# The feed-forward's projection back by seven products of sums, added up in shared PSUM banks

## The chip, the cores and the metric

The kernel runs on one core of one Trainium2 chip. The metric is the device time of one execution in microseconds (us); lower is better. All inputs and outputs are float32 in the chip's memory, and the kernel is one launch.

## The reference

One layer of a bidirectional encoder for 1024 tokens of width 1024: two token mixers, a SwiGLU feed-forward, a per-layer embedding, a final norm. What matters here is the feed-forward, with D_FF = 2816:

```python
h = rms_norm(x, g_ffn[i])
gt, up = split_cols(h @ w_gate_up[i], (D_FF, D_FF))
x = x + (jax.nn.silu(gt) * up) @ w_down[i]

pl = rms_norm(p[i] @ w_pl_proj[i], g_pl_proj[i])
x = x + jax.nn.sigmoid(rms_norm(x, g_pl[i]) @ w_pl_gate[i]) * pl
```

## The kernel before, in words

Everything is kept feature by token: a tile has 128 features on its partitions and 512 tokens (a token half) or 1024 along the free axis. To keep float32's precision, each operand is split into two float32r parts, hi and lo (`split`: ACT casts hi, DVE subtracts to get lo), and each 128x128 by 128x512 block is three products on TensorE: hi x hi, hi x lo, lo x hi (`mm3`). One PSUM bank holds one 128x512 result, and there are eight banks.

The block is written down as a list of instructions on stand-ins for tiles. `Plan.order` then gives them an order by list scheduling with estimated durations (which engine does what next, by level and place in the list, as inputs and buffers come free), and `Plan.run` issues them in that order. So no queue is written out by hand, and each engine runs its list strictly in order. Buffers are slots of pools: 32 large ones of 1024 columns (`big`), 8 and 4 of 512 (`mid`, `raw`), 6 for split weights (`w`, `N_W`), 8 banks.

Gate and up (`gate_up`, lines 1566 to 1602) already use Winograd's form of Strassen's product: the features, the tokens and the weights' columns (gate and up) are halves, and seven products of sums take the place of eight. Each of the 22 blocks of 128 hidden features takes seven products of four feature blocks (84 products on TensorE), each into a bank of its own; DVE then adds banks and intermediate results in SBUF (p1, u3, u4), ACT applies Silu, and the two token halves of the block go to memory (`d_hid`, 256 KB each). Block 0 is done plainly (`plain`), and blocks 1 to 4 have their first two products done early (`early`).

The projection back (`down`, lines 1640 to 1668) is plain. It runs over pieces of hidden blocks, `PIECES = (2, 4, 4, 1, 6, 5)`. For a piece it loads and splits both token halves of each block, then for each of eight 128-column blocks of the output loads and splits the weights (`load3`, four blocks to a tile) and, by token half, adds up the piece in one bank (`block_half`). DVE adds the bank to x, which stays in eight large tiles (`xT`). The last piece also splits x for the embedding and takes up its norm. Loads for this stage wait for the first half of hidden block 19 (`also=[d_hid[NF - 1 - X_AHEAD][0]]`).

While gate and up run, 28 of the 32 large slots hold the split sums of x; the first piece has two blocks because four slots are free before they end.

Of the kernel before, what the change touches and what calls it, by code (L numbers as in the profile page):

```python
# [14 lines left out]
F32R = mybir.dt.float32r  # L15
# [21 lines left out]
class Buf:  # L37
    """A stand-in for a tile."""
# [15 lines left out]
class View:  # L54
    """Part of a tile: partitions [p0, p1), free dimensions as (stride, size) from an offset."""
# [82 lines left out]
class Op:  # L138
# [7 lines left out]
# a DMA: from its issue to its data, and bytes in a microsecond  # L146
# [3 lines left out]
# from the end of an instruction to the start of one that needs it, by the engines of both  # L150
# [7 lines left out]
class VPool:  # L158
# [5 lines left out]
    def tile(self, shape, dtype=F32, tag=None, bufs=None, line=None, cap=99, stream=None):  # L164
        """line: tiles of a line are given out in the order of the program, at most cap at a time."""
# [7 lines left out]
class Plan:  # L173
# [11 lines left out]
    # -- recording  # L185
# [44 lines left out]
    # -- engines  # L230
    def matmul(self, out, lhsT, rhs, start, stop):
# [5 lines left out]
        o = self.add("pe", lambda: self.nc.tensor.matmul(out.ap(), lhsT.ap(), rhs.ap(), start=start, stop=stop),  # L237
# [96 lines left out]
    # -- scheduling  # L334
    def order(self):
# [6 lines left out]
        free_slots = {}     # (pool, tag) -> times at which slots come free  # L342
        queue = {}          # line -> tiles in program order
# [8 lines left out]
        wait = {e: [] for e in engs}       # heap by ready time: dependencies all scheduled  # L352
        avail = {e: [] for e in engs}      # heap by key: ready at the engine's time
# [19 lines left out]
        def slots_ready(o, now):  # L373
            """None when it can go now; else (time or None, (pool, tag))."""
# [20 lines left out]
        while len(done) < total:  # L395
# [43 lines left out]
            # worth the wait: something more urgent is about to be ready  # L439
# [62 lines left out]
    # -- issue  # L502
# [28 lines left out]
P = 128  # L531
# [25 lines left out]
# slots of each kind of tile, and what goes before what  # L557
# [4 lines left out]
PIECES = (2, 4, 4, 1, 6, 5)  # L562
# [17 lines left out]
# products of part 1 in order (k, q, v, g: glu, z, l: logits, p: per-layer embedding; with the head or  # L580
# block), and those that fill in
# [6 lines left out]
def ORDER(f):  # L588
    """The block up to the delta rule's end, in the order in which it is written down."""
# [10 lines left out]
def hybrid_block(tc, x, p, g_mix, w_in, conv_dw_w, conv_dw_b,  # L600
# [7 lines left out]
    big = pn.pool("big", N_BIG)          # 1024 columns and the padding of a convolution  # L608
    mid = pn.pool("mid", N_MID)          # 512 columns
# [30 lines left out]
    # ---------------------------------------------------------------- constants  # L640
# [46 lines left out]
    def load_w(w, r0, nk, c0, cap=4, pool=None):  # L687
        """nk blocks of 128 rows of w, 128 columns, split: by four blocks."""
# [17 lines left out]
    def mm3(ps, ah, al, bh, bl, start, stop):  # L706
        pn.matmul(ps, ah, bh, start, False)
        pn.matmul(ps, ah, bl, False, False)
        pn.matmul(ps, al, bh, False, stop)

    def block_half(w, acts, h, nk):
        """128 columns of w against 512 tokens: a bank of [column, token]."""
# [18 lines left out]
    def rows(r, n):  # L731
        """[P, n] values by token as a bank whose rows all hold them along the free axis."""
# [5 lines left out]
    def sums(acc, n):  # L738
        """Sums over partitions of acc's columns, token on the partition."""
# [5 lines left out]
    # ---------------------------------------------------------------- part 1  # L745
# [4 lines left out]
    # vectors by feature: rows of 128, transposed together  # L750
# [15 lines left out]
    # RMSNorm of x, transposed; x itself transposed  # L766
# [56 lines left out]
    # logits of decay and beta  # L823
    d_g = dp.tile([P, P], tag="dg", bufs=1)

    def logits():
# [26 lines left out]
        # log1p(e) = ln(u) - ((u - 1) - e) / u with u = 1 + e  # L853
# [135 lines left out]
    # ---------------------------------------------------------------- the delta rule  # L989
# [21 lines left out]
    def group(g):  # L1011
# [6 lines left out]
        for hh in range(2):  # L1018
# [14 lines left out]
            # by token: 1/|k|^2, |k|, and what the writes are scaled with  # L1033
# [7 lines left out]
            # decays between the tokens of a chunk: the direction that runs from partition to column has  # L1041
            # the sum of its logs <= 0, the other one >= 0
# [15 lines left out]
            # N (both directions in one matrix) and P  # L1058
# [23 lines left out]
        # inverses of the 32x32 diagonal blocks, one block to a partition  # L1082
# [35 lines left out]
    def head(g, hh, v, N, kT, nrm, b_, zt, ssq):  # L1118
        hd = 2 * g + hh
        # the inverses of 128x128 (eu: backward, forward) and their transposes (et: forward, backward)  # L1120
# [5 lines left out]
        for q4 in range(2):  # L1126
# [15 lines left out]
            # only the blocks beside the diagonal blocks are used of each product  # L1142
# [4 lines left out]
            # columns of px: blocks 0, 1, 2, 3, each in the direction that has it here  # L1147
# [17 lines left out]
        # v, scaled by |k|  # L1165
# [14 lines left out]
        # the chunks in order, both directions side by side  # L1180
# [585 lines left out]
```

## Time and profile before

| what | us |
|---|---|
| runs | 2145.12, 2142.41, 2143.38 |
| median of the runs | 2143.38 |
| profiled execution, first to last instruction (span) | 2144.9 |
| gate and up, from their first weights' load to the last weights' load | 1333.4 to 1730.6 |
| projection back, loads of its weights | 1737.2 to 1998.3 |

The profiled execution's own time is given as its span alone; it lies within the range of the runs. Line 237 is `matmul` and line 282 `_vec`, the helpers that record nearly every product and DVE instruction, and lines 259 and 266 are ACT's, so instructions are told apart by tile names: `ps` is a bank, `w` split weights, `big` a large tile, `raw` and `mid` weights as loaded or intermediate results, `m` and `lnb` intermediate results of 512 columns.

### The profile page before, as it was taken

The numbers are of one execution on the slowest core, as the hardware profiler recorded it, in microseconds if no ns is written. First come the engines' busy times: TensorE is split into PE (matmuls) and PEld (weight loads), VectorE is DVE, ScalarE is ACT, GpSimd is POOL, SyncE is SP. The second block draws the span as 40 slices with busy tenths as digits, with TensorE's granted clock in tenths as the row PEclk, the third lists the DMA queues.
The fourth block names the chain that finished last, engine by engine and source line by source line (L and its number), as shares of the span: only waits on it lengthen the run. The fifth ranks groups of instructions, "written<-read, shape, count | busy, mean of one in ns | idle before, by whom it ended". The sixth has DMA issues, their size and how long they took to land.

```text
span 2144.9 us, 29696 instructions
## 1 busy us (share of the span) xinstructions
PE 2094.7 (98%) x10434; PEld 1736.6 (81%) x10434; DVE 1606.4 (75%) x2621; ACT 1089.8 (51%) x2501; POOL 129.5 (6%) x203
## 2 busy tenths in 40 slices
PE   7999999999999999999999999999999999999998
PEld 5888788878888788878888888888888888888888
DVE  4488999977898989887687868786666667452676
ACT  6636656756656655767775435533323334121542
POOL 1000201110100111011100000000000000000000
PEclk9999999999999999999999999999999999999999
DMA  6233224522423422635468687432222227231253
GB/s 213 100 123 127 84 81 138 187 79 79 138 89 120 146 74 79 197 122 182 157 213 254 195 262 229 123 99 84 80 78 84 84 80 273 67 95 39 66 170 108
DMA packets 289077, 278.69 MB, mean 130 GB/s; under 512 B 17209, under 2 KB 217074, under 8 KB 288928
## 3 DMA queue, kind: packets, MB, share of 16 engines
q1 hardware_dynamic: 288928, 276.79, 40.3%
q8 instruction: 82, 1.34, 0.3%
q14 instruction: 67, 0.55, 0.1%
HBM read 198.02 MB, written 78.71 MB: 129 GB/s over the span
## 4 chain that ended last, share of the span: by engine, by line
PE 86%; ACT 7%; DVE 5%; issue 1%; DMA 1%; SPq 0%; POOL 0%; DVEq 0%; POOLq 0%; ACTq 0%
PE ps L237 84%; ACT big L259 4%; DVE big L282 3%; PE ps L242 2%; DVE mid L282 1%; ACT big L266 1%; ACT m L266 1%; DVE w L282 1%; ACT w L259 1%; DMA big<-in_x_dram 1%; DMA d<-mid 0%; ACT mid L266 0%; SPq L330 0%; ACT L266 0%; ACT mid L259 0%
## 5 line engine op out<-in xcount | busy, mean ns | idle before, releaser
L237 PE MATMUL ps<-big,w 128*128 128x512 f32 (+1 forms) x7524 | 1848.7, 399 | 0.9 <-ACT w L259 0.8
L237 PEld LDWEIGHTS ps<-big,w 128*128 128x128 f32 x7524 | 1383.4, 189 | 305.3 <-ACT w L259 1.2
L282 DVE SCALAR_TENSOR_TENSOR big<-big,cw 128x1024 f32<-128x1024 f32 x336 | 434.2, 1299 | 17.3 <-ACT big L266 12.3
L259 ACT CAST w<-raw 128x512 fp32r<-128x512 f32 (+2 forms) x340 | 198.3, 589 | 365.0 <-PE ps L237 288.4
L282 DVE TENSOR_TENSOR w<-raw,w 128x512 fp32r<-128x512 f32 (+2 forms) x340 | 221.6, 659 | 124.9 <-ACT w L259 119.3
L282 DVE TENSOR_TENSOR big<-ps,big 128x512 f32<-128x512 f32 (+1 forms) x132 | 89.9, 687 | 86.4 <-PE ps L237 76.2
L259 ACT CAST w<-mid 128x512 fp32r<-128x512 f32 x125 | 77.2, 621 | 149.5 <-PE ps L237 109.5
L282 DVE TENSOR_TENSOR w<-mid,w 128x512 fp32r<-128x512 f32 x125 | 85.9, 688 | 62.3 <-ACT w L259 61.6
L237 PEld LDWEIGHTS ps<-big 128*128 128x128 f32 x784 | 101.9, 195 | 16.1 <-issue 9.1
L237 PE MATMUL ps<-big 128*128 128x128 f32 (+1 forms) x784 | 107.2, 283 | 7.7 <-ACT big L259 5.1
L282 DVE TENSOR_TENSOR big<-big 128x512 fp32r<-128x512 f32 (+2 forms) x159 | 107.0, 707 | 8.7 <-ACT big L259 8.4
L259 ACT COPY big<-big 32x128 f32<-32x128 f32 (+1 forms) x264 | 102.5, 440 | 16.5 <-DVE big L282 12.5
L259 ACT COPY big<-ps 32x128 f32<-32x128 f32 (+3 forms) x162 | 66.8, 413 | 64.3 <-PE ps L237 55.0
L259 ACT CAST big<-big 128x512 fp32r<-128x512 f32 x120 | 69.9, 619 | 42.5 <-DVE big L282 21.3
L242 PE MATMUL ps<-ident,big 128*128 128x128 f32 (+1 forms) x432 | 72.0, 280 | 13.6 <-DMA big<-in_x_dram 9.3
L237 PEld LDWEIGHTS ps<-S,big 128*128 128x128 f32 x448 | 71.8, 190 | 10.0 <-DVE S L282 0.2
L237 PE MATMUL ps<-S,big 128*128 128x128 f32 x448 | 75.0, 275 | 0.0
L242 PEld LDWEIGHTS ps<-ident,big 128*128 128x128 f32 (+1 forms) x432 | 53.9, 147 | 25.2 <-issue 13.4
L237 PEld LDWEIGHTS ps<-big,m 128*128 128x128 f32 x512 | 64.1, 195 | 12.2 <-ACT m L266 9.4
L237 PE MATMUL ps<-big,m 128*128 128x128 f32 x512 | 66.1, 280 | 6.4 <-ACT m L266 6.3
L266 ACT ACTIVATE mid<-mid 128x512 f32<-128x512 f32 (+2 forms) x87 | 50.2, 580 | 38.6 <-DVE mid L282 26.8
L266 ACT ACTIVATE big<-big 128x1024 f32<-128x1024 f32 (+2 forms) x80 | 56.6, 715 | 22.2 <-DVE big L282 17.2
(158 smaller groups left out, 1711.0 us busy)
## 6 DMA issues: line engine op xcount, KB each, us to landing
d<-mid SPq DMA_DIRECT2D x162, 256.0 KB, 3.0
raw<-in_w_in_dram SPq DMA_DIRECT2D x128, 256.0 KB, 3.0
mid<-d SPq DMA_DIRECT2D x120, 256.0 KB, 3.4
big<-d SPq DMA_DIRECT2D x92, 256.0 KB, 4.0
big<-dqkv SPq DMA_DIRECT2D x32, 512.0 KB, 4.9
raw<-in_w_gate_up_dram SPq DMA_DIRECT2D x50, 256.0 KB, 2.9
dqkv<-big SPq DMA_DIRECT2D x24, 512.0 KB, 2.9
mid<-in_w_gate_up_dram SPq DMA_DIRECT2D x46, 256.0 KB, 4.0
```

Source lines behind the costliest of these rows:

```text
L237: o = self.add("pe", lambda: self.nc.tensor.matmul(out.ap(), lhsT.ap(), rhs.ap(), start=start, stop=stop), [out], [lhsT, rhs], cost)
L242: self.add("pe", lambda: self.nc.tensor.transpose(out.ap(), in_.ap(), ident.ap()), [out], [in_, ident], 0.107)
L259: return self.nc.scalar.copy(out.ap(), in_.ap())
L266: return self.nc.scalar.activation(out.ap(), in_.ap(), func, **kw)
L282: return getattr(e, name)(**{k: v.ap() if isinstance(v, View) else v for k, v in kw.items()})
```

## The change

The projection back takes the seven products too, for hidden blocks 0 to 17 as nine pairs (`NS = 9`), in three groups of three pairs (`PAIRS = (3, 3, 3)`); blocks 18 to 21 stay plain, as the last piece. The halves are the even and odd blocks of the pairs (features), the token halves, and two neighbouring 128-column blocks of the output.

- `hidden`: when both blocks of a pair are done, DVE takes four differences in place, and the seven forms (11, T1, T2, 21, T3, 22, T4) go to memory, 256 KB each, where four halves went before.
- `down_sums`: per group, 7 x 3 forms are loaded and split into large tiles (`df`, at most 24), then for four pairs of output blocks the four weight parts (three blocks, 384 columns) are loaded, four sums of weights are taken, and seven split weights give seven products of nine TensorE products each.
- Shared banks: T2, T3 and T4 are added into the bank that holds product 11, and 22 into that of T1. Between two products into one bank DVE adds it to x (`onto`): seven additions per pair.
- `gate_up` for blocks 5 to 21 shares banks in the same way (four banks, `pb`, `pc`, `pd` and none for the rest): ACT copies `pb` out three times between its products, and the additions on DVE that the bank now makes are left out.

```diff
-PIECES = (2, 4, 4, 1, 6, 5)
+PAIRS = (3, 3, 3)
+NS = sum(PAIRS)
+HID_CAP, DF_CAP = 3, 24
...
+    def hidden(fb):
+        if fb >= 2 * NS:
+            t = hid.pop(fb)
+            for h in range(2):
+                pn.dma(d_hid[fb][h], t[:, h])
+        elif fb % 2:
+            a, b = hid.pop(fb - 1), hid.pop(fb)
+            o11, o12, o21, o22 = a[:, 0], a[:, 1], b[:, 0], b[:, 1]
+            d = d_form[fb // 2]
+            pn.dma(d["22"], o22)
+            pn.dma(d["11"], o11)
+            pn.tt(o11, o12, o11, ALU.subtract)
+            pn.dma(d["T1"], o11)
+            pn.tt(o12, o22, o12, ALU.subtract)
+            pn.dma(d["T3"], o12)
+            pn.tt(o22, o22, o11, ALU.subtract)
+            pn.dma(d["T2"], o22)
+            pn.dma(d["21"], o21)
+            pn.tt(o21, o21, o22, ALU.subtract)
+            pn.dma(d["T4"], o21)
...
+        t1 = split_w(a11)
+        pb = gu_bank()
+        for k in range(HK):
+            mm3(pb, t1[:, 0, k], t1[:, 1, k], *B11[k], k == 0, k == HK - 1)
...
+        pn.act(p1, pb)
+        pn.tt(s, a21, a22, ALU.add)
+        pc = product(s, T1)
...
+        product(s, T2, pb)
...
+        pn.act(g1, pb)
...
+        pd = product(a12, B21)
+        pn.tt(g0, pd, p1, ALU.add)
+        pn.act(g0, g0, AF.Silu)
+        product(a21, T3, pb)
+        u4 = medium(line="gw", cap=2)
+        pn.act(u4, pb)
+        pn.tt(u4, pc, u4, ALU.add)
         pn.tt(a12, a12, s, ALU.subtract)
-        p3 = product(a12, B22)
-        if early:
-            p6 = product(s, T2)
-        pn.tt(p1, p6, p1, ALU.add)
-        u3, u4 = medium(line="gv", cap=2), medium(line="gw", cap=2)
-        pn.tt(u3, p7, p1, ALU.add)
-        pn.tt(u4, p5, u3, ALU.add)              # up, second half
-        pn.tt(p1, p5, p1, ALU.add)
-        pn.tt(p1, p3, p1, ALU.add)              # gate, second half
-        pn.act(p1, p1, AF.Silu)
-        pn.tt(u4, u4, p1, ALU.mult)
-        pn.dma(d_hid[fb][1], u4)
-        pn.tt(u3, product(a22, T4), u3, ALU.add)  # up, first half
-        pn.tt(u3, u3, g0, ALU.mult)
-        pn.dma(d_hid[fb][0], u3)
+        product(a12, B22, pc)
+        pn.tt(g1, pc, g1, ALU.add)
+        pn.act(g1, g1, AF.Silu)
+        t = hid_tile(fb)
+        pn.tt(t[:, 1], u4, g1, ALU.mult)
+        product(a22, T4, pb)
+        pn.tt(t[:, 0], pb, g0, ALU.mult)
+        hidden(fb)
...
+    def down_sums(p0, n):
...
+        for name in FORMS:
+            acts[name] = []
+            for i in range(n):
+                acts[name].append(hid_form(d_form[p0 + i][name], [d_late]))
...
+        def onto(b, h, ps):
+            v = xT[b][:, hs(h)]
+            pn.tt(v, ps, v, ALU.add)
...
+        for b in range(0, KB, 2):
+            a11, a21 = part_d(2 * p0, n, 0, b, "raw"), part_d(2 * p0, n, 0, b + 1, "raw")
+            a22, a12 = part_d(2 * p0, n, 1, b + 1, "rawb"), part_d(2 * p0, n, 1, b, "rawb")
...
+            s = medium(line="gs", cap=2)[:, :n * P].fold(n, P)
+            pb = product(a11, "11")
+            onto(b, 0, pb)
+            pn.tt(s, a21, a22, ALU.add)
+            pc = product(s, "T1")
+            onto(b + 1, 1, pc)
+            pn.tt(s, s, a11, ALU.subtract)
+            pn.tt(a21, a11, a21, ALU.subtract)
+            product(s, "T2", pb)
+            onto(b, 1, pb)
+            pd = product(a12, "21")
+            onto(b, 0, pd)
+            pn.tt(a12, a12, s, ALU.subtract)
+            product(a21, "T3", pb)
+            onto(b + 1, 1, pb)
+            product(a12, "22", pc)
+            onto(b, 1, pc)
+            product(a22, "T4", pb)
+            onto(b + 1, 0, pb)
...
-    f0 = 0
-    for n in PIECES:
-        down(f0, n)
-        f0 += n
+    d_late = d_hid[NF - 1 - X_AHEAD][0]
+    p0 = 0
+    for n in PAIRS:
+        down_sums(p0, n)
+        p0 += n
+    down(2 * NS, NF - 2 * NS)
```

What the scheduler makes of it is seen in three places.

PE before, in the piece of six blocks: 18 products go into one bank, then the next 18 into another; the first row of each waits for its weights.

```order
L237 MATMUL ps_17302<-big_16413,w_17231 128x512 [waits DVE_49,Activation_49]
L237 MATMUL ps_17302<-big_16413,w_17231 128x512 x2
L237 MATMUL ps_17302<-big_16546,w_17231 128x512 x3
L237 MATMUL ps_17302<-big_16561,w_17231 128x512 x3
L237 MATMUL ps_17302<-big_16842,w_17231 128x512 x3
L237 MATMUL ps_17302<-big_16857,w_17258 128x512 [waits Activation_49]
L237 MATMUL ps_17302<-big_16857,w_17258 128x512 x2
L237 MATMUL ps_17302<-big_16867,w_17258 128x512 x3
L237 MATMUL ps_17334<-big_16419,w_17231 128x512 [waits DVE_49]
L237 MATMUL ps_17334<-big_16419,w_17231 128x512 x2
L237 MATMUL ps_17334<-big_16555,w_17231 128x512 x3
```

PE now, in the third pair of output blocks of the first group (ps_16636 is the bank of product 11, ps_16684 that of 21, ps_16652 that of T1):

```order
L239 MATMUL ps_16636<-big_16229,w_16591 128x512 [waits DVE_49,Activation_49]
L239 MATMUL ps_16636<-big_16229,w_16591 128x512 x2
L239 MATMUL ps_16636<-big_16238,w_16591 128x512 x3
L239 MATMUL ps_16636<-big_16243,w_16591 128x512 x3
L239 MATMUL ps_16684<-big_16248,w_16608 128x512 [waits Activation_49]
L239 MATMUL ps_16684<-big_16248,w_16608 128x512 x2
L239 MATMUL ps_16684<-big_16252,w_16608 128x512 x3
L239 MATMUL ps_16684<-big_16264,w_16608 128x512 x3
L239 MATMUL ps_16636<-big_16270,w_16622 128x512 [waits DVE_49,Activation_49]
L239 MATMUL ps_16636<-big_16270,w_16622 128x512 x2
L239 MATMUL ps_16636<-big_16276,w_16622 128x512 x3
L239 MATMUL ps_16636<-big_16282,w_16622 128x512 x3
```

Nine products follow each other in a bank, and PE comes back to ps_16636 after nine products elsewhere, each time with a wait for DVE, which has to read the bank between.

PE now, in gate and up (ps_14975 is the bank of product 11, T2, T3 and T4 of one block, ps_15036 that of T1 and 22, ps_15116 the next block's first bank):

```order
L239 MATMUL ps_15116<-big_12731,w_15057 128x512 x2
L239 MATMUL ps_15116<-big_12731,w_15057 128x512 [waits DVE_49]
L239 MATMUL ps_15116<-big_12743,w_15057 128x512 x2
L239 MATMUL ps_14975<-big_13392,w_15043 128x512 [waits Activation_49]
L239 MATMUL ps_14975<-big_13392,w_15043 128x512 x2
L239 MATMUL ps_15036<-big_13097,w_15022 128x512 [waits DVE_49]
L239 MATMUL ps_15036<-big_13097,w_15022 128x512 x2
L239 MATMUL ps_15036<-big_13102,w_15022 128x512 x3
L239 MATMUL ps_15036<-big_13110,w_15022 128x512 x3
```

Five products of the next block stand between T3 and T4 in bank ps_14975, three of T4 follow, then 22 goes into ps_15036 after DVE's read of it.

DVE now, in the first pair of the second group (big_16867 to big_16895 are forms, ps_16954 is the bank of product 21, w_16893 the split weights of T3, whose low half PE reads from T3's third product on):

```order
L284 TENSOR_TENSOR big_16867<-big_16867 128x512 [waits DMAHW0_49,Activation_49]
L284 TENSOR_TENSOR mid_16661<-mid_16661,mid_16669 128x384 [waits DVE_49]
L284 TENSOR_TENSOR big_16874<-big_16874 128x512 [waits DMAHW1_49,Activation_49]
L284 TENSOR_TENSOR big_16880<-big_16880 128x512 [waits DMAHW2_49,Activation_49]
L284 TENSOR_TENSOR big_16079<-ps_16954,big_16079 128x512 [waits PE_49]
L284 TENSOR_TENSOR big_16887<-big_16887 128x512 [waits DMAHW3_49,Activation_49]
L284 TENSOR_TENSOR w_16893<-raw_16633,w_16893 128x384
L284 TENSOR_TENSOR w_16973<-mid_16661,w_16973 128x384 [waits DVE_49]
```

The low half of T3's weights now stands behind a run of forms' low halves and of bank additions; before, a piece had at most twelve such forms, and none of its weights had a sum to wait for.

## Rows read from the trace of the kernel before

**Rows 1.** The page: span, busy time of the engines, TensorE's granted clock by slice.

```profile
span 2144.9 us, 29696 instructions
...
PE 2094.7 (98%) x10434; PEld 1736.6 (81%) x10434; DVE 1606.4 (75%) x2621; ACT 1089.8 (51%) x2501; POOL 129.5 (6%) x203
...
PEclk9999999999999999999999999999999999999999
```

**Rows 2.** Chain of waits, in order of time: start us, us, what.

```profile
1097.79 984.46 PE ps L237 x4257
2083.01 3.20 PE ps L237 x27
```

**Rows 3.** Who waited for whom, PE, 1100 to 2145 us: total us, times, longest.

```profile
PE ps L242 <- DVE big L282: 1.7, 1, 1.7
```

**Rows 4.** Windows: gate and up, the passage, the projection back; columns in the first line.

```profile
core 0: us, PE busy (x) PEld busy (x) DVE busy (x) ACT busy (x) POOL busy (x), PEclk, DMA share, GB/s
1500.00:1540.00 40.00, 40.00 (x173) 32.22 (x172) 26.30 (x41) 12.48 (x21) 0.00 (x0) 1.00 0.26 79
1780.00:1820.00 40.00, 40.00 (x173) 32.18 (x172) 37.40 (x63) 21.11 (x39) 0.00 (x0) 1.00 0.75 256
1940.00:1980.00 40.00, 40.00 (x173) 32.19 (x172) 11.41 (x20) 4.82 (x10) 0.00 (x0) 1.00 0.14 42
```

**Rows 5.** Timeline of DVE, piece of six blocks: start us, us, engine, line, operation.

```profile
1925.56 0.69 DVE L282 TENSOR_TENSOR big<-ps,big 128x512 f32<-128x512 f32 x1
...
1942.38 0.69 DVE L282 TENSOR_TENSOR big<-ps,big 128x512 f32<-128x512 f32 x1
```

**Rows 6.** Timeline of DVE, gate and up; four like rows lie between.

```profile
1508.60 0.68 DVE L282 TENSOR_TENSOR m<-ps,m 128x512 f32<-128x512 f32 x1
...
1511.59 0.68 DVE L282 TENSOR_TENSOR mid<-mid,m 128x512 f32<-128x512 f32 x1
```

**Rows 7.** Groups by shape, 1500 to 2145 us: count, busy us, mean ns, idle before.

```profile
L282 DVE TENSOR_TENSOR big<-ps,big 128x512 f32<-128x512 f32 x96 | 65.3, 688 | 74.3 <-PE ps L237 73.4
...
L259 ACT COPY m<-ps 128x512 f32<-128x512 f32 x18 | 10.6, 587 | 27.3 <-PE ps L237 27.3
...
L282 DVE TENSOR_TENSOR w<-raw,w 128x256 fp32r<-128x256 f32 x16 | 6.7, 419 | 6.4 <-ACT w L259 4.1 <-DMA big<-d 2.4
```

**Rows 8.** Windows with the most DMA; DMA issues: KB each, median us to landing.

```profile
1775.00:1780.00 5.00, 5.00 (x23) 4.05 (x22) 0.73 (x3) 0.55 (x2) 0.00 (x0) 1.00 1.06 395
...
big<-d SPq DMA_DIRECT2D x92, 256.0 KB, 4.0
...
d<-big SPq DMA_DIRECT2D x32, 256.0 KB, 2.1
```

**Rows 9.** Timeline near the end: PE to DVE, then DVE to PE.

```profile
2081.61 0.63 PE L237 MATMUL ps<-big,w 128*128 128x512 f32 x2
...
2082.28 0.69 DVE L282 TENSOR_TENSOR mid<-ps,m 128x512 f32<-128x512 f32 x1 [0.16 <-PE ps L237]
...
2135.22 0.43 DVE L282 TENSOR_TENSOR big<-big,mid 128x256 f32<-128x256 f32 x1
2135.70 0.96 PEld L242 LDWEIGHTS ps<-ident,big 128*128 128x128 f32 x9 [1.97 <-DVE big L282]
```

**Rows 10.** Windows before, in and without a fall of the clock; PE's timeline between.

```profile
1020.00:1027.00 7.00, 4.12 (x24) 3.09 (x24) 3.67 (x7) 6.93 (x20) 1.64 (x1) 1.00 0.19 56
1027.00:1033.00 6.00, 4.71 (x20) 4.42 (x21) 2.85 (x7) 2.74 (x8) 0.21 (x1) 0.63 0.59 200
...
2120.00:2136.00 16.00, 14.26 (x122) 14.03 (x121) 9.19 (x22) 2.67 (x7) 0.00 (x0) 1.00 0.20 61
...
1028.29 1.87 PE L237 MATMUL ps<-big,m 128*128 128x128 f32 x8 [2.39 <-ACT m L266]
```

More of the change, by code (lines that the diff above doesn't have):

```diff
@@ L138 @@
 class Op:
+    pass
 TABLES = {AF.Exp: 0, AF.Sigmoid: 1, AF.Silu: 2, AF.Ln: 3}
@@ L228, in add, with matmul @@
         return o
-    def matmul(self, out, lhsT, rhs, start, stop):
+    def matmul(self, out, lhsT, rhs, start, stop, more=False):
+        kw = {"skip_group_check": True} if more else {}
         n = rhs.n
@@ L236, in matmul @@
             cost = 2 * max(0.107, n / 1200)
-        o = self.add("pe", lambda: self.nc.tensor.matmul(out.ap(), lhsT.ap(), rhs.ap(), start=start, stop=stop),
+        o = self.add("pe", lambda: self.nc.tensor.matmul(out.ap(), lhsT.ap(), rhs.ap(), start=start, stop=stop, **kw),
                      [out], [lhsT, rhs], cost)
@@ L704, in load_w, with mm3 @@
         return parts
[L706 to L709, printed above, removed]
+    def mm3(ps, ah, al, bh, bl, start, stop, more=False):
+        pn.matmul(ps, ah, bh, start, False, more)
+        pn.matmul(ps, ah, bl, False, False, more)
+        pn.matmul(ps, al, bh, False, stop, more)
     def block_half(w, acts, h, nk):
@@ L1522, in hybrid_block, with hid_tile @@
                 parted(B21, k, quarter(1, 0)[k])
-    d_hid = [[spill() for _ in range(2)] for _ in range(NF)]
+    FORMS = ("11", "T1", "T2", "21", "T3", "22", "T4")
+    d_form = [{n: spill() for n in FORMS} for _ in range(NS)]
+    d_hid = {fb: [spill() for _ in range(2)] for fb in range(2 * NS, NF)}
+    hid = {}
+    def hidden(fb):
[18 more added lines that the diff above has]
+            pn.dma(d["T4"], o21)
+    def hid_tile(fb):
+        hid[fb] = large([P, 2, HW], line="hid", cap=HID_CAP)
+        return hid[fb]
     def part_w(r, c, line):
@@ L1540, in product @@
         for k in range(HK):
-            mm3(ps, t[:, 0, k], t[:, 1, k], *acts[k], k == 0, k == HK - 1)
+            mm3(ps, t[:, 0, k], t[:, 1, k], *acts[k], k == 0 and onto is None, k == HK - 1, onto is not None)
         return ps
@@ L1638, in hybrid_block, with x_of, hid_form, part_d @@
     xT = [None] * KB
+    def x_of(b):
+        xT[b] = large(line="xT")
+        for i in range(2):
+            pn.dma(xT[b][:, hs(i)], d_x2[b][i], also=[d_late])
+    def hid_form(d, also=()):
+        t = large([P, 2, HW], F32R, line="df", cap=DF_CAP)
+        hi, lo = t[:, 0], t[:, 1]
+        pn.dma(lo.f(), d, also=also)
+        split(hi, lo, lo.f())
+        return hi, lo
+    def part_d(f0, n, r, b, line):
+        t = mid.tile([P, HK, P], tag="raw", bufs=4, line=line, cap=4, stream="rest") if line == "raw" else \
+            mid.tile([P, HK, P], tag="mid", line=line, cap=4)
+        rows_ = w_down[0][f0 * P:(f0 + 2 * n) * P, b * P:(b + 1) * P]
+        pn.dma(t[:, :n], rows_.rearrange("(k r q) c -> r q k c", r=2, q=P)[r])
+        return t[:, :n]
@@ new lines, in down_sums, with product @@
+    def down_sums(p0, n):
+        pn.sec = "down"
+        if p0 == 0:
+            x_of(0)
+            x_of(1)
+        acts = {}
+        for name in FORMS:
+            acts[name] = []
+            for i in range(n):
+                acts[name].append(hid_form(d_form[p0 + i][name], [d_late]))
+        def product(src, name, ps=None):
+            t, more = wp.tile([P, 2, HK, P], F32R, tag="w", line="w", cap=N_W, stream="rest"), ps is not None
+            split(t[:, 0, :n], t[:, 1, :n], src)
+            ps = ps or gu_bank()
+            for k in range(n):
+                mm3(ps, t[:, 0, k], t[:, 1, k], *acts[name][k], k == 0 and not more, k == n - 1, more)
+            return ps
+        def onto(b, h, ps):
[4 more added lines that the diff above has]
+            a22, a12 = part_d(2 * p0, n, 1, b + 1, "rawb"), part_d(2 * p0, n, 1, b, "rawb")
+            if xT[b] is None:
+                x_of(b)
+                x_of(b + 1)
+            s = medium(line="gs", cap=2)[:, :n * P].fold(n, P)
[4 more added lines that the diff above has]
+            onto(b + 1, 1, pc)
+            pn.tt(s, s, a11, ALU.subtract)
+            pn.tt(a21, a11, a21, ALU.subtract)
+            product(s, "T2", pb)
+            onto(b, 1, pb)
+            pd = product(a12, "21")
+            onto(b, 0, pd)
+            pn.tt(a12, a12, s, ALU.subtract)
+            product(a21, "T3", pb)
[4 more added lines that the diff above has]
+            onto(b + 1, 0, pb)
@@ L1640, in down @@
     def down(fb, n):
         pn.sec = "down"
-        first, last = fb == 0, fb + n == NF
+        last = fb + n == NF
         acts = []
@@ L1646, in down @@
             for h in range(2):
-                hi, lo = half_pair()
-                pn.dma(lo.f(), d_hid[fb + k][h], also=[d_hid[NF - 1 - X_AHEAD][0]])
-                split(hi, lo, lo.f())
-                acts[k].append((hi, lo))
+                acts[k].append(hid_form(d_hid[fb + k][h]))
         def fn(b, h, w):
             ps = block_half(w, lambda k, h: acts[k][h], h, n)
-            if first and h == 0:
-                xT[b] = large(line="xT")
-                for i in range(2):
-                    pn.dma(xT[b][:, hs(i)], d_x2[b][i], also=[d_hid[NF - 1 - X_AHEAD][0]])
             v = xT[b][:, hs(h)]
```

43 lines of the change are left out of this document (28 added, 15 removed).

## The prediction

> **What bounds the kernel now.** I read the page first. Over the whole span TensorE is busy 98% of the time and its clock is at the upper of its two levels in every slice [rows 1]. Such a share can still hide a stage with another limit, so next comes the chain of waits: from 1097.79 us it is one unbroken piece on PE of 984.46 us, through the output projection, gate and up, the projection back, and into the embedding [rows 2]. The third view, who waited for whom from 1100 us on, has one line for PE, 1.7 us, and it lies at the very end [rows 3]. The windows say the same by stage: PE fills 40.00 of 40 us in gate and up, at the passage to the projection back, and inside that projection, while DVE goes from 26.30 to 37.40 to 11.41 us of 40 [rows 4]. So the part that is changed is bound by the number of products that PE issues, and DVE is the engine that could come to bind: it is close to full at one place already.
>
> What a product costs is read from where PE waits for nothing. In the piece of six blocks DVE adds up a bank after every 18 products; four such steps take 16.82 us [rows 5], so 72 products take 16.82 us: 0.2336 us each.
>
> **The products removed.** Before, the projection back has 22 blocks x 8 column blocks x 2 token halves x 3 products = 1056. After, each pair of 128-column output blocks needs seven products over nine block pairs of three products each: 4 x 7 x 9 x 3 = 756, and the last four blocks 4 x 8 x 2 x 3 = 192, together 948. 108 products x 0.2336 = **25.2 us less on PE**. Gate and up keep their number, and the engines' orders are the same, row for row, up to the first blocks of gate and up. Without new waits the span would be 2144.9 - 25.2 = 2119.7.
>
> **What is added.** DVE instructions of 512 columns that stand close together start 0.60 us apart (2.99 us for five steps) [rows 6], though one lasts 0.68 to 0.69. For the new 384-column ones I have no row. One of 256 lasts 0.419 and one of 512 0.688 [rows 7]; the middle is 0.55, less the same overlap 0.47 (an estimate; the ends are 0.42 and 0.60).
>
> *Gate and up.* A normal block had 20 DVE instructions (7 low halves of weights, 4 sums of weights, 9 of banks and intermediate sums). It has 16 now, plus 4 differences for each pair of blocks: 18 x 0.60 = 10.8 us in the 84 x 0.2336 = 19.6 us that PE needs. Two more ACT copies of 0.587 us [rows 7] fall to an engine busy 12.48 of 40 [rows 4]. I cost all of it at nothing, and PE's 84 products are the cover. The 27 more stores and 27 more loads of 256 KB, 14 MB in some 550 us, meet a DMA share of 0.26 [rows 4]; it has moved 395 GB/s with PE still full [rows 8]. A difference that overwrites a part waits for that part's store (2.1 us to landing [rows 8]); DVE has 8.8 us idle per block to spend on that.
>
> *The shared banks.* Here PE must not add to a bank until ACT or DVE has read it. The price of one such turn: after a product 0.04 us to DVE, the read 0.69, 0.05 us to PE [rows 7, 9], plus 0.16 because a product lasts 0.40 (two last 0.63 [rows 9]) while the next starts after 0.23: 0.94 us. In the projection back nine products into another bank lie between, 2.10 us; DVE may be 1.1 us behind before PE stands. In gate and up the tightest turn has five products between, 1.17 us, for an ACT copy of 0.587: 0.9 with its handoffs. Behind it DVE adds that copy to the neighbouring bank, 1.7 us in all against eight products, 1.87. Bounds: nothing at the lower end, and 0.3 us a block for 17 blocks, 5 us, at the upper, if each handoff is 0.2 us longer than the rows. I take nothing, since these rows are of the same engines.
> Sharing banks has a rule against it. The Trainium skill (PSUM — Partial Sum Buffer, section "PSUM bank collisions raise a hardware error") asks that two engines be kept apart by whole bank, so every read here is a wait in PE's order and never an overlap. By that rule alone, with nothing between, each turn would cost 0.94 us. No row before has such a turn to agree or differ.
>
> *The projection back.* The work of a group of three pairs on DVE is 21 low halves of forms and 28 bank additions at 0.60, 28 low halves of weights and 16 sums at 0.47: 29.4 + 20.7 = 50.1 us, against 252 products = 58.9 us on PE. It fits on average. It is not even, though: the forms fall due in the first pair, where PE needs all 21 within 14.7 us.
> Entry. From the end of the last block's fourth product to the first group's T4 product DVE's order has 24 long and 9 short instructions, 18.6 us; PE has 90 products, 21.0. No stall, 2.4 us to spare, close to the 37.40 of 40 that DVE does there now.
> Group 1 to 2. From the end of the last pair's T2 product to the low half of the weights of T3 (w_16893) DVE has 26 long and 6 short: 18.4 us. Going down the rows it also waits 1.3 us for banks that PE still fills, and 0.4 are handoffs: 20.1. PE has 80 products, 18.7. PE stands **1.4 us**.
> Group 2 to 3. By the same count 25 long and 6 short, 17.8, with 0.6 of waiting and 0.3 of handoffs 18.8, against 72 products, 16.8: **2.0 us**.
> Bounds for the two boundaries: 0 where a DVE instruction goes a little faster, and 2 x 18 forms x 0.60 = 21.6 where no form is prepared before the old group has ended. I take 3.4. What is late next there is nothing else: the forms' slots come free from the first product of the last pair on, 14.7 us before use, against 4.0 us to landing [rows 8].
> *The last piece* has four blocks instead of five. Per column block PE has 24 products, 5.6 us; DVE's three operations per half and one weight half come to some 4.5. Nothing.
>
> **Sum:** 2144.9 - 25.2 + 3.4 = 2123.1 by the profiled execution. The runs' median, 2143.38, is 1.5 below that span, so the forecast is 2121.6, with half a microsecond for small stands **2122**.
>
> **The rivals.**
> *Forms late, or the DVE fuller than I count.* Half of the 21.6 us at the boundaries, and a few tenths at turns: 2143.4 - 25.2 + 11 + 2 = 2131. For it: DVE is full for 20 us at each boundary, so any delay there is PE's. Against it: PE's products are the slower part elsewhere. 0.12.
> *The clock falls.* In the trace the granted clock fell to a mean of 0.63 for 6 us after PE had been busy only 4.12 of 7 us, with a stand of 2.39; with PE busy 14.26 of 16 it stayed at 1.00 [rows 10]. My stands are of the second kind. If it fell at all three passages it would cost (1 - 0.63) x 6 = 2.2 us each: 2122 + 6.6 = 2129. 0.05. The Trainium skill (TensorE: Matmul & The Clock Gate, section "A second HAM failure mode: psum-queue depth-cycling") has a kernel whose small idles between banks brought the clock down; here the second kind of row speaks against it.
> *DVE late at the turns of the banks (slower).* A pair has three turns with 2.10 us of cover, 36 in all. To eat 25.2 us and be 4.3 us slower, with 3.4 at the boundaries, each must run 0.72 us over, so DVE must stand 1.9 us behind at every turn, three instructions or more. Then 2148. For it: in-order DVE has weights and forms between the additions. Against: a pair away from boundaries has 7 x 0.60 + 11 x 0.47 = 9.4 us on DVE against 14.7, two instructions between additions. 0.05.
> *The gain does not come*, within 0.2%, by half of that: 2143. 0.04. That the products aren't removed is excluded by the order, which has 108 fewer.
>
> **How the numbers follow.** My forecast, 2117 to 2126, has 0.74. Below it lies 2117 (all 25.2 us and no stand is 2118.2 from the median). The range runs on through the first two rivals to 2131; left out are the two dear ones and the far ends. 0.2% is 4.3 us, about what a measurement of this kernel can tell from no change: faster is below 2139.1, 0.74 + 0.12 + 0.05 = 0.91; same 0.04; slower 0.05.
>
> **What would show it.** In the profile after: one long PE piece again, some 22 us shorter, with the spacing of products still 0.233 to 0.234; stands of PE of 0.4 to 1.6 us, waiting for DVE's `w`, once in the first pair of the second and of the third group, none in gate and up; DVE near full for 20 us around them. If PE shows regular waits for `ps` reads in every pair, the slower rival holds; if the stands wait for `big` or DMA, the forms are late; if PE is short of work in gate and up, the turns there are dearer than the rows say. A time above 2131 would mean that one of these was sized wrong.

## The result, and the profile after

The changed kernel takes **2119.98 us** (median of 2120.64, 2121.71, 2119.33 and 2118.43), against 2144.04 for the kernel before beside it: a ratio of 0.9889, 95% interval 0.9875 to 0.9903. The forecast was 2122, 2117 to 2131. One execution of e1 below and one of the kernel before beside it lasted 4183 us; the ratios leave both out, and e1's median, which counts its own, would be 2142.99 without it. Line numbers of the helpers are two higher now: 239 is `matmul`, 284 `_vec`, 261 and 268 are ACT's, 332 the DMAs.

The page after, against [rows 1]:

```profile
span 2118.9 us, 29685 instructions
...
PE 2068.0 (98%) x10326; PEld 1714.5 (81%) x10326; DVE 1650.1 (78%) x2696; ACT 1137.0 (54%) x2590; POOL 130.4 (6%) x203
...
PEclk9999999999999999999999999999999999999999
```

PE works 26.7 us less and stays at 98%; DVE has 43.7 us more work and ACT 47.2. The chain of waits, from its long piece on (start us, us, what), against [rows 2]:

```profile
1093.88 737.92 PE ps L239 x3174
1831.82 4.91 DMA big<-d
...
1836.79 6.23 DMA big<-d
...
1851.51 45.65 PE ps L239 x194
...
1907.41 149.18 PE ps L239 x662
...
2057.36 3.19 PE ps L239 x27
```

The piece that was unbroken is broken twice now, near 1840 and near 1900 us, where DVE and DMA pieces lie in the chain: the passages from group 1 to 2 and from 2 to 3. From the start of the long piece to the start of the x27 piece in the embedding went 985.22 us before and 963.48 go now: **21.7 less**. I call this stretch the changed part and compare by it below. What lies ahead of it has the same instructions in the same order, and was 3.9 us shorter in this execution (1093.88 for 1097.79). Over the profiles of all fourteen kernels it ends between 1091.17 and 1099.82, so I put that down to the execution and not to the change; why it varies wasn't tried.

Who PE waited for in the changed part (total us, times, longest); before there was nothing [rows 3]:

```profile
PE ps L239 <- DVE w L284: 0.9, 1, 0.9
PE ps L239 <- ACT w L261: 0.6, 1, 0.6
PE ps L239 <- DVE big L284: 0.4, 1, 0.4
```

Windows in gate and up, at the entry into the projection back, ahead of the first boundary, and at the two boundaries, against [rows 4]:

```profile
core 0: us, PE busy (x) PEld busy (x) DVE busy (x) ACT busy (x) POOL busy (x), PEclk, DMA share, GB/s
1500.00:1540.00 40.00, 40.00 (x173) 32.20 (x172) 24.16 (x37) 14.18 (x25) 0.00 (x0) 1.00 0.33 103
1780.00:1800.00 20.00, 20.00 (x87) 16.15 (x86) 18.60 (x35) 10.16 (x21) 0.00 (x0) 1.00 0.87 306
1830.00:1840.00 10.00, 10.00 (x44) 8.07 (x43) 9.21 (x17) 6.90 (x14) 0.00 (x0) 1.00 1.01 352
1840.00:1860.00 20.00, 18.97 (x80) 14.53 (x80) 19.50 (x36) 11.14 (x22) 0.00 (x0) 1.00 0.49 168
1900.00:1920.00 20.00, 19.07 (x82) 14.92 (x81) 19.97 (x37) 11.21 (x22) 0.00 (x0) 1.00 0.44 151
```

Gate and up and the entry have PE full. At the boundaries DVE works 19.50 and 19.97 of 20 us, and 80 and 82 products are recorded where a full window has 87. The clock stays at 1.00. That the first boundary is DVE's, and no late transfer, stands in DVE's own waits from 1836 to 1852 us: it only waited for banks, three times, and for no DMA, though a form now takes 5.1 us to land (4.0 in [rows 8]).

```profile
DVE big L284 <- PE ps L239: 0.6, 3, 0.2
```

The transfers are not far behind, though: the chain ahead of the first boundary holds two landings of forms, of 4.91 and 6.23 us, up to 1843.02, and from 1830 to 1840 us the DMA share is 1.01. Whether they would bind next with much less work on DVE, no run here shows.

The new operation, 384 columns on DVE (two in 1.02 us, so 0.47 from one to the next):

```profile
1852.27 1.02 DVE L284 TENSOR_TENSOR w<-mid,w 128x384 fp32r<-128x384 f32 x2
```

### The profile page after: what moved, and what is told of

Same layout as the page of the kernel before. It is cut to its first block, busy times and chain, and to the rows that moved or that the text cites. A ratio compares the mean times of both kernels' runs of the same rounds, so it can differ in the third digit from the quotient of the medians.

```text
span 2118.9 us, 29685 instructions
## 1 busy us (share of the span) xinstructions
PE 2068.0 (98%) x10326; PEld 1714.5 (81%) x10326; DVE 1650.1 (78%) x2696; ACT 1137.0 (54%) x2590; POOL 130.4 (6%) x203
## 4 chain that ended last, share of the span: by engine, by line
PE 84%; ACT 7%; DVE 5%; DMA 2%; issue 1%; SPq 0%; DVEq 0%; POOLq 0%; POOL 0%; ACTq 0%
PE ps L239 82%; ACT big L261 4%; DVE big L284 3%; PE ps L244 2%; DVE mid L284 1%; ACT big L268 1%; ACT m L268 1%; DMA big<-in_x_dram 1%; DVE w L284 1%; ACT w L261 1%; DMA big<-d 1%; DMA d<-mid 0%; SPq L332 0%; ACT mid L268 0%; ACT L268 0%
## 5 line engine op out<-in xcount | busy, mean ns | idle before, releaser
L239 PE MATMUL ps<-big,w 128*128 128x512 f32 (+1 forms) x7416 | 1823.7, 399 | 2.9 <-ACT w L261 1.4
L239 PEld LDWEIGHTS ps<-big,w 128*128 128x128 f32 x7416 | 1362.0, 189 | 303.4 <-ACT w L261 2.4
L261 ACT CAST w<-raw 128x512 fp32r<-128x512 f32 (+2 forms) x308 | 184.6, 605 | 274.2 <-PE ps L239 216.0
L284 DVE TENSOR_TENSOR w<-raw,w 128x512 fp32r<-128x512 f32 (+2 forms) x308 | 208.2, 682 | 74.4 <-ACT w L261 72.6
L261 ACT CAST w<-mid 128x512 fp32r<-128x512 f32 (+1 forms) x185 | 107.4, 586 | 166.2 <-PE ps L239 104.5
L284 DVE TENSOR_TENSOR big<-big 128x512 fp32r<-128x512 f32 (+2 forms) x222 | 149.5, 702 | 11.0 <-ACT big L261 7.9
L284 DVE TENSOR_TENSOR w<-mid,w 128x512 fp32r<-128x512 f32 (+1 forms) x185 | 118.4, 644 | 44.8 <-ACT w L261 44.0
L284 DVE TENSOR_TENSOR big<-ps,big 128x512 f32<-128x512 f32 (+1 forms) x146 | 100.3, 688 | 43.1 <-PE ps L239 33.2
L261 ACT CAST big<-big 128x512 fp32r<-128x512 f32 x147 | 85.8, 619 | 40.6 <-DVE big L284 24.0
L261 ACT COPY mid<-ps 128x512 f32<-128x512 f32 x81 | 47.0, 588 | 70.2 <-PE ps L239 57.4
```

The lines of the kernel that those rows point to most:

```text
L261: return self.nc.scalar.copy(out.ap(), in_.ap())
L284: return getattr(e, name)(**{k: v.ap() if isinstance(v, View) else v for k, v in kw.items()})
```

## The experiments

All start from the changed kernel. "Part" is the changed part's length less the 963.48 of the changed kernel; "stands" is what the view of waits gives for PE in that part (1.9 us in the changed kernel). Both are of the one profiled execution, the medians of all: e11's lasted 2131.05 us and e12's 2124.79, above their medians, and most of that lies ahead of the part (it starts at 1099.82 and 1097.52).

| run | edit | median us | ratio to before, 95% | part | stands |
|---|---|---|---|---|---|
| e1 | projection back plain | 2143.28 | 0.9982 to 1.0004 | +22.1 | 0 |
| e2 | own banks in gate and up | 2127.38 | 0.9907 to 0.9937 | +5.1 | 5.6 |
| e3 | two groups only | 2127.90 | 0.9910 to 0.9941 | +7.1 | 1.0 |
| e4 | bare turns | 2173.34 | 1.0122 to 1.0165 | +52.6 | 43.9 |
| e5 | own banks in the projection back | 2132.71 | 0.9936 to 0.9961 | +12.7 | 9.7 |
| e6 | weights first | 2131.13 | 0.9922 to 0.9949 | +8.4 | 6.3 |
| e7 | sums on GpSimd | 2120.87 | 0.9878 to 0.9905 | 0.0 | 0.9 |
| e8 | no form ahead | 2134.17 | 0.9939 to 0.9964 | +10.6 | 7.3 |
| e9 | e2, one sum first | 2127.60 | 0.9904 to 0.9932 | +5.3 | 5.7 |
| e10 | forms on GpSimd | 2121.28 | 0.9882 to 0.9909 | +1.3 | 3.2 |
| e11 | e2, last block early | 2123.14 | 0.9899 to 0.9926 | +4.0 | 4.9 |
| e12 | last block early | 2120.72 | 0.9893 to 0.9923 | +0.5 | 2.3 |

**e1: is it the products?**

```diff
-PAIRS = (3, 3, 3)
+PAIRS = ()
+PIECES = (2, 4, 4, 1, 6, 5)
...
+    f0 = 0
+    for n in PIECES:
+        down(f0, n)
+        f0 += n
```

> The projection back plain for all 22 blocks in pieces of 2, 4, 4, 1, 6, 5 as before, gate/up unchanged with its shared banks. Theory (the gain is 108 products at 0.2336 us, less two stands of some 3 us together; the shared banks of gate/up are worth nothing): 2120 + 25.2 - 3 = 2142 us, within 0.2% of the kernel before. Rival 1 (the shared banks of gate/up, which take 2 of 20 additions per block from VectorE, carry part of the gain): 2138 us or less. Rival 2 (they cost time, which the products hide in the changed kernel): 2147 us or more.

The pieces' loads wait for hidden block 19 again, as before. 2143.28, as the theory said; the chain is one piece again:

```profile
1096.75 984.79 PE ps L239 x4257
...
2082.31 3.19 PE ps L239 x27
```

985.56 us from start to start, as before. So the shared banks of gate and up alone are worth nothing, and the whole gain comes with the projection back.

**e3: by how many?** `PAIRS = (3, 3)` and the other ten blocks plain, 5 and 5.

> Two groups of three pairs by seven products, the other ten blocks plain in two pieces of five. Theory: 36 products more at 0.2336 us = +8.4, and one of two stands of 1 to 2 us less: 2120 + 8.4 - 1.5 = 2127 us (2126 to 2128.5). Rival (the third group's saving is used up by its stand and by VectorE): 2121 us or less.

2127.90, part +7.1: 36 x 0.2336 = 8.4, less 1.3 for the one boundary that is gone (0.9 of it a stand by name). The third group pays as counted.

**e4: what does a turn of a bank cost?** The order of the products in a pair (three sums of weights are taken ahead of them, and the bank of 21, now last, needs a sum more per pair; a pair has 63 products here, the expectation's 84 is gate and up's number):

```diff
+            pn.strict = True
             pb = product(a11, "11")
             onto(b, 0, pb)
...
+            product(s1, "T2", pb)
+            onto(b, 1, pb)
+            product(a21, "T3", pb)
+            onto(b + 1, 1, pb)
+            product(a22, "T4", pb)
+            onto(b + 1, 0, pb)
```

> The same 84 products per pair, in an order in which each product that is added onto a bank comes right behind the one before on that bank, so that nothing covers VectorE's read: 4 bare turns for each two blocks of columns, 48 in all. Theory (a turn is 0.94 us from the last product to the next: handoff 0.04, addition some 0.7, handoff 0.05, and the first product's pipeline): 48 x 0.94 = +45 us, 2165 us (2155 to 2172). Rival 1 (TensorE goes on into a bank while it is read): 2120 us. Rival 2 (a turn also empties the queue of TensorE and costs over 1.3 us): 2182 us or more.

2173.34: 53.4 us over the changed kernel for 48 turns, **1.11 us each**; rival 1 is out, and rival 2's 1.3 us is not reached. The timeline of a pair of turns:

```profile
1802.92 2.33 PE L244 MATMUL ps<-big,w 128*128 128x512 f32 x9 [0.87 <-DVE big L289]
...
1805.29 0.69 DVE L289 TENSOR_TENSOR big<-ps,big 128x512 f32<-128x512 f32 x1 [0.86 <-PE ps L244]
...
1806.13 2.33 PE L244 MATMUL ps<-big,w 128*128 128x512 f32 x9 [0.87 <-DVE big L289]
```

Nine products start 3.21 us after the nine before, for 2.10 us of work. DVE starts 0.04 us behind the last product and ends at 1805.98, and PE starts at 1806.13, so this handoff is 0.15 us where I had read 0.05 [rows 9]. With the addition's 0.69 that is 0.88; the other 0.23 is in PE's nine products, which last 2.33 us with the last one's tail. In e6 below an addition out of a bank and the next product are only some 0.05 apart, so 0.15 isn't the price of every such handoff; what makes it longer here isn't settled. With 2.10 us of other products between, as in the change, even 1.11 us is covered.

Behind four of seven products PE stands some 0.87 us here, for 60 us on end, and the clock stays at 1.00:

```profile
1860.00:1920.00 60.00, 48.42 (x195) 35.82 (x196) 38.59 (x71) 14.19 (x28) 0.00 (x0) 1.00 0.22 65
```

In the kernel that the Trainium skill tells of (TensorE: Matmul & The Clock Gate, section "A second HAM failure mode: psum-queue depth-cycling") small idles between banks brought the clock down. This run doesn't agree with that for stands of 0.87 us.

**e5: what do the shared banks of the projection back spare?**

```diff
-            product(s, "T2", pb)
-            onto(b, 1, pb)
...
+            pn.tt(u, product(s, "T2"), u, ALU.add)
+            onto(b, 1, u)
```

> The projection back by seven with a bank of its own for every product: the running sum is kept in SBUF, 11 additions on VectorE and a copy on ScalarE for each two blocks of columns in place of 7 additions. Theory (VectorE is what the stands wait for): per group VectorE goes from 4 x 9.3 + 21 x 0.6 = 50 us to 4 x 11.7 + 12.6 = 59.5 us, against 58.9 us of TensorE, so the stands at the two boundaries grow by 1 to 3 us each: 2123 us (2121 to 2127). Rival (the reads between two products on one bank cost time now): faster than the changed kernel, 2118 us or less.

2132.71: the direction of the theory, four times its size. PE stands 7.8 us more where I expected 2 to 6, and the part is 12.7 longer, 4.9 more than the stands explain. That difference comes back in e8.

**e8 and e6: the boundary made worse.** e8 has `DF_CAP = 21` for 24; e6 gives loads, sums and splitting of the weights level 0.45 for 1.0.

> 21 slots for forms in place of 24: no form of the next group is loaded before one of this group is done. Theory (VectorE's load in the two pairs around a boundary makes the stands): 3 forms of 0.6 us more per boundary, +1.8 us each, 2123.5 us (2122 to 2125). Rival (landing makes them; the three first forms are not the ones that wait): 2120 to 2121 us.

> The weights of the seven products (load, sums, splitting) get a more urgent level in the planner than the forms of the next group, so that the first weights of a group are ready ahead of the forms. Theory (the stands are VectorE's order and load at a boundary): half to all of the 2.8 us that TensorE stands there goes, 2117.3 to 2119 us. Rival (the stands are the landing of the forms, some 5.1 us per DMA at a boundary): 2120 us or later.

e8 is 2134.17, far over what either theory gave. PE's waits in the changed part:

```profile
PE ps L239 <- ACT w L261: 7.3, 2, 3.7
```

Windows behind the first stand, columns as above:

```profile
1850.00:1855.00 5.00, 5.00 (x12) 3.85 (x13) 3.70 (x8) 2.21 (x6) 0.00 (x0) 0.50 0.15 43
1855.00:1860.00 5.00, 5.00 (x23) 4.04 (x22) 4.01 (x9) 0.47 (x2) 0.00 (x0) 1.00 0.29 80
```

Two stands of 3.7 us, 5.4 us more than in the changed kernel, and behind the first the granted clock is at 0.50, the lower level: 12 products in 5 us where the next 5 us have 23 (13 and 23 behind the second). The part is 10.6 longer: 5.4 of stands, and some 5 behind them at the lower clock, where the two windows hold 11 and 10 products too few (21 x 0.2336 = 4.9). In e5 the same difference is 4.9 and in e6 4.0, and there too windows behind the stands fall to 0.50 and 0.66. In e2, e9 and e11, further down, 5 us behind the longest stands (3.9, 3.2 and 3.1 us) show 0.66. In e7, e10, e12 and the changed kernel, whose longest stands are 0.4, 1.6, 0.9 and 0.9 us, no window at a boundary is below 1.00.

e6 came out at 2131.13: slower, as its rival had it, but not by landing. The timeline at its longest stand:

```profile
1858.83 3.67 DVE L284 TENSOR_TENSOR big<-ps,big 128x512 f32<-128x512 f32 x6
1859.56 6.71 PE L239 MATMUL ps<-big,w 128*128 128x512 f32 x21 [2.63 <-DVE big L284]
```

Weights and forms went first, six additions out of banks stood behind them, and PE goes on when the first of the six is done: the turn of a bank, late on DVE, which I had as the slower rival, at both boundaries (2.6 and 2.4 us). So moving one kind of DVE work ahead makes another late; the planner's order in the changed kernel was the better one.

**e2, e9, e11, e12: why do own banks in gate and up cost 7 us here, and nothing in e1?**

> Gate/up with a bank for each of the seven products, as before; the projection back as changed. Theory: VectorE has 11 to 13 us of work in 20 us of gate/up, two more additions of 0.6 us per block are hidden: 2120 us, within 1.5. Rival (the lighter VectorE of gate/up is what lets the forms of the first group be ready in time): a stand at the entry of the projection back, 2123 us or more.

2127.38; the theory fell. The rival had the place wrong: the entry has no stand, the first boundary has 4.7 us of them. PE's waits from 1835 to 1880 us:

```profile
PE ps L239 <- ACT w L261: 3.9, 1, 3.9
PE ps L239 <- DVE w L284: 0.8, 2, 0.4
```

My first guess was one weight sum that stood behind the forms. e9 moves it ahead:

```diff
+            pn.level = 0.45
             pn.tt(s, s, a11, ALU.subtract)
+            pn.level = 1.0
```

> As e2 (own banks in gate/up), but the difference s - a11 of the weights (128x384, 0.47 us on VectorE) has a more urgent level in the planner: at the first boundary it moves ahead of six low halves of forms, where it stood behind them in e2. Nothing else is asked for. Theory (e2 lost its 7 us because this one sum stood behind the forms: a stand of 3.9 us in place of some 1, and on top of it the granted clock at 0.5 for some us after it): 2121 us (2119.5 to 2123). Rival (it is the additions of gate/up themselves, or VectorE's sum of work): 2126 to 2128 us, as e2.

2127.60: nothing. The sum came earlier, and the low half of its weights was then late. The guess fell as e6's did. What the timeline of DVE shows is another thing, in e2 and then in the changed kernel:

```profile
1827.15 0.68 DVE L284 TENSOR_TENSOR big<-ps,m 128x512 f32<-128x512 f32 x1
...
1828.48 0.68 DVE L284 TENSOR_TENSOR m<-ps,m 128x512 f32<-128x512 f32 x1
...
1829.67 0.68 DVE L284 TENSOR_TENSOR m<-ps,m 128x512 f32<-128x512 f32 x1
1830.27 0.68 DVE L284 TENSOR_TENSOR big<-big,lnb 128x512 f32<-128x512 f32 x1
...
1831.47 0.69 DVE L284 TENSOR_TENSOR big<-big,m 128x512 f32<-128x512 f32 x1
...
1834.72 0.69 DVE L284 TENSOR_TENSOR big<-ps,big 128x512 f32<-128x512 f32 x1 [0.30 <-PE ps L239]
...
1849.01 0.56 DVE L284 TENSOR_TENSOR mid<-mid,raw 128x384 f32<-128x384 f32 x1
```

```profile
1827.29 0.69 DVE L284 TENSOR_TENSOR big<-mid,m 128x512 f32<-128x512 f32 x1
1827.89 0.68 DVE L284 TENSOR_TENSOR big<-ps,lnb 128x512 f32<-128x512 f32 x1
...
1835.24 0.55 DVE L284 TENSOR_TENSOR mid<-mid,raw 128x384 f32<-128x384 f32 x1
```

`m` and `lnb` are gate and up's tiles. The last block of gate and up ends here, some 45 us into the projection back, since its results go into a large tile, and 24 forms and eight tiles of x hold all 32. What it still has to do on DVE then falls right ahead of the first boundary: seven operations with own banks (two more are among the `big<-ps,big` rows), two with shared ones. 5 x 0.60 = 3.0 us more, and the stands grew by 3.7.

The last row of each timeline shows what they displace: the sum that e9 moved (`s - a11` of the next group's first pair) is taken at 1835.24 in the changed kernel and at 1849.01 in e2, behind the forms, and PE's stand of 3.9 us ends right behind its cast. DVE isn't simply 3.0 us late: at 1834.72 it still waits for a bank. The operations push the weights behind the forms in the planner's order, and e9 brought only one of them forward, by some 5 us (1848.64 in a profile whose part starts 4.3 us later).

e11 and e12 write the results of the four plain blocks into 512-column tiles, with own and with shared banks (e11's edit):

```diff
+        if fb >= 2 * NS:
+            u3, u4 = medium(line="gv", cap=1), medium(line="gw", cap=1)
+        else:
+            t = hid_tile(fb)
+            u3, u4 = t[:, 0], t[:, 1]
```

> As e2 (own banks in gate/up), but the four blocks that are projected back plainly write their two results into tiles of 512 columns, as the kernel before did, not into a large tile; so the last block of gate/up no longer waits for a large tile until the first group's forms give one back, and its seven last operations on VectorE come at the end of gate/up, not right at the first boundary. Theory (e2 lost its time because the last block ends at the boundary, with 7 operations of 0.6 us in place of 2 in the changed kernel; 5 x 0.6 = 3.0 us of stand, and the clock falls on top): 2119 us (2117.5 to 2121). Rival (own banks cost by themselves, in all blocks): 2126 us or more.

> The changed kernel with that one edit: the four plain blocks' results in tiles of 512 columns. Theory: 2 operations of 0.6 us less on VectorE at the first boundary, its stand (some 1 us) goes or halves, the second stays: 2118 to 2119.5 us. Rival (the same operations now make the entry into the first group late, where VectorE was 18.6 of 20 us busy): 2121 us or more.

e11, 2123.14, lies between its two theories, and its profile says why. By window, first 1760 to 1835, then 1835 to 1880 us:

```profile
PE ps L239 <- DVE big L284: 3.1, 1, 3.1
```

```profile
PE ps L239 <- DVE w L284: 0.9, 1, 0.9
```

The first boundary is down to 0.9 us (1.0 in the changed kernel), so the place was right. But the seven operations now lie ahead of the entry, and there is the stand, 3.1 us. With shared banks (e12, 2120.72) the same move gives 0.5 at the entry, and 0.9 at each boundary: no gain.

**e7 and e10: DVE's work to GpSimd.** e7 gives it the four sums of weights of each pair, e10 the low half of every third form; e10 also gives the planner a longer estimate for GpSimd.

```diff
-            pn.tt(s, a21, a22, ALU.add)
+            pn.tt(s, a21, a22, ALU.add, eng="pool")
...
-        split(hi, lo, lo.f())
+        pn.act(hi, lo.f())
+        pn.tt(lo, lo.f(), hi.f(), ALU.subtract, eng=eng)
```

> The four sums and differences of weights for each two blocks of columns (128x384) on GpSimd in place of VectorE, 48 in all. Theory (VectorE's load makes the stands): VectorE loses 48 x 0.47 = 22.6 us, 3.7 of it around each boundary, the stands go: 2117 to 2118 us. Rival 1 (DMA landing makes them): 2120 us. Rival 2 (GpSimd takes longer than the 0.47 us of VectorE or slows VectorE, and the weights come late in every pair): 2123 us or more.

> The low half of every third form (128x512, 7 of 21 in each group) on GpSimd in place of VectorE. Theory (the two stands are VectorE's load at the boundaries): 7 x 0.6 = 4.2 us less on VectorE just there, GpSimd has 7 x some 1.55 us (by the 1.14 to 1.24 us of its 128x384 in e7) of the 20 us, the stands shrink to under 1 us together: 2117 to 2118.5 us. Rival (GpSimd's forms come late, or the stands move to the next late instruction as in e7): 2120 us or more.

2120.87 and 2121.28: no gain from either, though DVE has 48 or 21 operations fewer. The groups of DVE and GpSimd from 1775 to 1925 us, in the changed kernel, in e7 and in e10:

```profile
L284 DVE TENSOR_TENSOR big<-ps,big 128x512 f32<-128x512 f32 x66 | 45.5, 689 | 16.6 <-PE ps L239 16.2
L284 DVE TENSOR_TENSOR big<-big 128x512 fp32r<-128x512 f32 x59 | 38.6, 685 | 0.0
```

```profile
L284 DVE TENSOR_TENSOR big<-ps,big 128x512 f32<-128x512 f32 x66 | 45.3, 687 | 24.3 <-PE ps L239 24.1
L284 DVE TENSOR_TENSOR big<-big 128x512 fp32r<-128x512 f32 x60 | 43.3, 753 | 0.0
...
L284 POOL TENSOR_TENSOR mid<-mid 128x384 f32<-128x384 f32 x10 | 12.9, 1288 | 36.7 <-DVE w L284 21.6 <-issue 12.3 <-DMA raw<-in_w_down_dram 2.8
```

```profile
L284 DVE TENSOR_TENSOR big<-ps,big 128x512 f32<-128x512 f32 x64 | 43.8, 685 | 18.1 <-PE ps L239 17.8
L284 DVE TENSOR_TENSOR big<-big 128x512 fp32r<-128x512 f32 x42 | 31.3, 749 | 0.0
...
L284 POOL TENSOR_TENSOR big<-big 128x512 fp32r<-128x512 f32 x20 | 31.9, 1593 | 123.2 <-ACT big L261 119.6 <-PE ps L239 2.6 <-DVE big L284 1.0
```

DVE's instructions that read two tiles in SBUF grew from 685 to 753 and 749 ns in the mean; those that read a bank stayed at 685 to 689. One pair in e10's timeline:

```profile
1841.83 0.68 DVE L284 TENSOR_TENSOR big<-ps,big 128x512 f32<-128x512 f32 x1
1842.43 1.05 DVE L284 TENSOR_TENSOR w<-mid,w 128x384 fp32r<-128x384 f32 x1
...
1843.62 1.49 POOL L284 TENSOR_TENSOR big<-big 128x512 fp32r<-128x512 f32 x1 [0.55 <-ACT big L261]
1843.87 1.78 DVE L284 TENSOR_TENSOR big<-big 128x512 fp32r<-128x512 f32 x1
```

The DVE operation at 1843.87 usually lasts 0.68; it took 1.78 and ended 0.54 us behind GpSimd's, which had started just ahead of it. The Trainium skill (SBUF — State Buffer, section "Who interferes with whom") says that a VectorE instruction with two inputs in SBUF and a GpSimd instruction that reads SBUF contend, since the second input comes through a read interface that the two share, and that such sharing is an exclusive lock; these rows agree. Much of what DVE gave away came back that way: over these 150 us it has 20 instructions fewer in e10 and is busy 131.1 us for 132.6. In e7 it has 36 fewer and is busy 124.7. There the named stands are halved (0.9 for 1.9) without a gain in the part, and the same 150 us hold 631 products for 632, so PE lost as much as before, in pieces too short for that view. What they wait for isn't settled.

## Why the prediction was right, point by point

- **The products removed**, -25.2 us: right. e1, which has them all again and no group boundary, adds 22.1 us to the part; the 3.1 between are close to what the boundaries lose below. e3 gives the same price for 36 of them.
- **The boundaries**, +3.4 (1.4 and 2.0): the part fell by 21.7 of 25.2, so 3.5 were lost. The view of waits names 1.9 of it; the windows, with 7 and 5 products too few, put 1.6 at the first boundary and 1.2 at the second, 2.8 together. The other 0.7 isn't placed. So the sum agrees better than its terms: the first was about right, the second, 2.0, too dear, and that the whole came to 3.5 is in part luck. I had named DVE's `w` for both; at the first it was a cast of ACT behind DVE's sum of weights (0.6) and a form (0.4).
- **The entry**: no stand, and DVE worked 18.60 of 20 us. e11 shows how little room there was: with own banks, the last block's operations there cost 3.1 us.
- **Turns of the shared banks**, 0.94 us against 2.10 of cover: costed at nothing, and right. The turn itself is 1.11 in e4; 0.10 of the 0.17 that I had too small is the handoff from DVE to PE there.
- **384 columns on DVE**, 0.47 by estimate: 0.47.
- **Gate and up costed at nothing**: right for the steady blocks (DVE 24.16 and ACT 14.18 of 40 us, PE 40.00). I missed that the last block ends at a boundary. There the sharing spares 7.4 us by the medians, 5.1 of them in the part (e2), which stood in no term of the sum.
- **The clock's rival**, 2129 at 0.05: it didn't come, but both it and "forms late", 2131, lie nearer than their chances say. Four small edits (e2, e5, e6, e8) land at 2127 to 2134, by stands of 2.4 to 5.9 us and a fallen clock behind them. I had these as two rivals; the first brings the second.
- **2.3 us of the 24.1** between the medians are not in the changed part; they are within what the stretch ahead of it varies by. They are why the time is 2 us below the forecast, and nothing in the prediction accounts for them.

None of the twelve has a lower median than the changed kernel.

## What to carry to other kernels

Where PE is full, products left out are worth their count times their spacing, and the rest is a count of the in-order engine behind it at the few places where its work bunches: entry, group boundaries, and whatever the planner pushed there. Look for work of an earlier stage that waits for a buffer and so ends at such a place; five operations that cost nothing in the stage itself cost 5 us of the part there, 7 in the medians. And treat a stand of some microseconds as dearer than its length, since the clock may fall behind it, as it did in six runs here: in e8 5.4 us more of stands cost 10.6.

## What was not expected of the hardware

A handoff from DVE to PE of 0.15 us between an addition out of a bank and the next product (e4), three times what the embedding's rows had shown, while e6 has some 0.05 at the same place. GpSimd's two-input operations (1.2 to 1.3 us for 384 columns, 1.6 for 512) stretch DVE's SBUF instructions, but not those that read a bank (e7, e10). The clock stayed at 1.00 through 45 stands of at most 1.8 us behind one another (e4) and through single ones of 1.6 (e10), and stood at 0.50 behind stands of 3.7 (e8); behind the 2.6 of e6, which follows a stand of 0.7 by 2.7 us, 5 us show 0.66.
